# A float32 transpose of 8192 by 8192: buffers split three and two, a looped TensorE, and ScalarE as the issuer

## The chip, the core and the metric

The kernel runs on one core of one Trainium2 chip. The core has a matrix engine (TensorE, PE in the profile), VectorE (DVE), ScalarE (ACT), GpSimd (POOL) and SyncE (SP), each with its own queue of instructions, and 16 DMA engines that move data between the chip's memory (HBM) and the on-chip memory (SBUF). TensorE writes into accumulators (PSUM). The metric is the time of one execution on the device in microseconds, lower is better.

## The reference

```python
"x": np.random.randn(8192, 8192).astype(np.float32)
...
return np.transpose(x)
```

268.4 MB are read and 268.4 MB are written. There is no arithmetic; all of the work is to move data and to turn it.

## The kernel before

The input is cut into 128 chunks, numbered t: two strips of 4096 columns, and in each strip 64 groups of 128 rows. One load brings a chunk, 128 rows by 4096 columns (2 MB), into a unit of SBUF. A unit is 16 pieces of 256 columns; a piece is transposed by two TensorE instructions of 128 by 128, so a chunk is 32 transposes into PSUM, whose two halves (`pss[0]`, `pss[1]`) hold eight pieces each. ScalarE empties the first half and VectorE the second.

A transposed chunk would give output rows that are only 512 bytes long. So the output is put together over 16 chunks. The 16 pieces of a chunk belong to 16 ranges of output rows, numbered q. In step t the range q = t mod 16 is closed: the pieces that chunks t-15 to t have for this range (a window) are brought side by side into a final buffer, and one store of 2 MB writes them, 8 KB a row. Pieces that wait for their range to close lie in `slots`. The first 15 windows, and those at the change from one strip to the other, are shorter or come as two stores; after the last chunk 15 closing windows are left, which are gathered from slots and stored.

SBUF has room for five units. Before the change they are three final buffers (NF = 3) and two load buffers (NIN = 2); the last final buffer takes load 2 at the start and becomes a final buffer from t = 4 on. The work is ordered as follows.

- TensorE (lines 205 to 224) has 28 transposes of the identity ahead of the first chunk (line 207), and then, written out chunk after chunk, the ranges in a turned order: first the range that closes in this step, then the one that closes in the next.
- ScalarE copies the first of these straight from PSUM to the final buffer of this step (line 232) and the second straight to the final buffer of the next step (line 245). Then it copies the other six pieces of its half to slots (line 266).
- VectorE, in step t, first copies its half to slots and, ahead of that in its queue, gathers the 14 older pieces of the window that closes in step t+1 (line 255). A gather waits until the store that used this final buffer before has landed.
- SyncE issues every load and every store (lines 122, 177 and 179). The store of step t waits for ScalarE's first copy (`s_last`) and the gather; a load waits until TensorE has finished the chunk that was in its buffer (line 275).
- After the last chunk, ScalarE and VectorE gather the 15 closing windows in turns (line 288), and SyncE issues their stores.

Of the kernel before, what the change touches and what calls it, by code (L numbers as in the profile page):

```python
# [40 lines left out]
def kernel(  # L41
# [28 lines left out]
    NF = 3  # L70
    NIN = 2
    WARM = 28

    with tc.tile_critical():  # L74
# [7 lines left out]
        s_ld = [nc.alloc_semaphore(f"s_ld{k}") for k in range(NIN + 1)]  # L82
        s_st = [nc.alloc_semaphore(f"s_st{k}") for k in range(NF + NIN)]
        s_pe = nc.alloc_semaphore("s_pe")
        s_last = nc.alloc_semaphore("s_last")
        s_cp = [nc.alloc_semaphore("s_cpa"), nc.alloc_semaphore("s_cpv")]
        s_ga = [nc.alloc_semaphore("s_gaa"), nc.alloc_semaphore("s_gav")]

        chunks = [(s, c) for s in range(M // J) for c in range(CH)]
        T = len(chunks)  # L90
# [12 lines left out]

        def unit(k):
            return units[:, k * UNIT:(k + 1) * UNIT]

        where = []
        for t in range(T):
            if t == NIN:
                where.append((unit(NF - 1), s_ld[NIN], 16))  # L110
            else:
                k = (t if t < NIN else t + 1) % NIN
                n = sum(w[1] is s_ld[k] for w in where)
                where.append((unit(NF + k), s_ld[k], 16 * (n + 1)))
        after = [None] * T
        for t in range(NIN + 1, T):
            after[t] = max(u for u in range(t) if where[u][1] is where[t][1])

        def load(t):
            s, c = chunks[t]  # L120
            dst, sem, _ = where[t]
            nc.sync.dma_start(
                out=dst, in_=x[c * P:(c + 1) * P, s * J:(s + 1) * J]
            ).then_inc(sem, 16)
# [25 lines left out]
        def move(e, o, i):  # L150
            return nc.scalar.copy(out=o, in_=i) if e == 0 else nc.vector.tensor_copy(out=o, in_=i)  # L151


        free = list(range(NF - 1))
# [14 lines left out]
        def store(w):  # L169
            q, r, parts, _, _ = w  # L170
            for s, a, z, base in parts:
                rows = (z - a) * P
                j0 = s * J + q * B * P
                dst = out[j0:j0 + B * P, a * P:z * P].rearrange("(p b) i -> p b i", p=P)
                src = units[:, base:base + B * rows]
                if any(stored):
                    st = wide_dma(nc, nc.sync, "qSPDynamicHW", dst, src)
                else:
                    st = nc.sync.dma_start(
                        out=dst, in_=src.rearrange("p (b i) -> p b i", b=B)  # L180
                    )
                st.then_inc(s_st[r], 16)
                stored[r] += 1
            free.append(r)
# [3 lines left out]
        def gather(e, w, members):  # L188
            eng = (nc.scalar, nc.vector)[e]
            q, r, _, place, before = w  # L190
# [9 lines left out]
        def closing(t):  # L200
            return window(t % W, max(0, t - W + 1), t) if t < T else None

        for t in range(NIN + 1):
            load(t)
        nc.tensor.wait_ge(s_id, 2)
        for k in range(WARM):
            nc.tensor.transpose(pss[1][:, :P], ident, ident)  # L207

        now = closing(0)
        marks = (2, W // 2, W)  # L210
        for t in range(T):
            src, sem, count = where[t]
            nc.tensor.wait_ge(sem, count)
            for i in range(W):
                if t and i % (W // 2) == 0:
                    nc.tensor.wait_ge(s_cp[2 * i // W], t)
                for b in range(B):
                    o = (i % (W // 2) * B + b) * P
                    j = (t + i) % W * PIECE + b
                    tr = nc.tensor.transpose(  # L220
                        pss[2 * i // W][:, o:o + P], src[:, j:j + B * (P - 1) + 1:B], ident
                    )
                if i + 1 in marks:
                    tr.then_inc(s_pe, 1)


            q, r, parts, place, before = now
            if before:
                nc.scalar.wait_ge(s_st[r], before)
            nc.scalar.wait_ge(s_pe, len(marks) * t + 1)  # L230
            off, dist = place[t]
            move(0, view(units, off, 0, 1, dist), view(pss[0], 0, 0, 1, P)).then_inc(s_last, 1)
            need = gathered[1]
            nxt = None
            if t + 1 < T:
                if t + 1 == NIN + 2:
                    free.append(NF - 1)
                while not free:
                    raise RuntimeError
                nxt = closing(t + 1)  # L240
            if nxt:
                if nxt[4]:
                    nc.scalar.wait_ge(s_st[nxt[1]], nxt[4])
                off, dist = nxt[3][t]
                move(0, view(units, off, 0, 1, dist), view(pss[0], PIECE, 0, 1, P))


            if nxt:
                members = [u for u in nxt[3] if u < t]
                if members:  # L250
                    if nxt[4]:
                        nc.vector.wait_ge(s_st[nxt[1]], nxt[4])
                    for k in range(2):
                        nc.vector.wait_ge(s_cp[k], t)
                    gather(1, nxt, members)


            for e in range(2):
                eng = (nc.scalar, nc.vector)[e]
                if need:  # L260
                    eng.wait_ge(s_ga[1], need)
                lo, hi = ((1 if nxt is None else 2), W // 2) if e == 0 else (W // 2, W)
                eng.wait_ge(s_pe, len(marks) * t + 2 + e)  # L263
                pairs = [(slot(t, t + i), (i - e * (W // 2)) * PIECE) for i in range(lo, hi)]
                for a, b, da, db, k in runs(pairs):
                    mv = move(e, view(slots, a, da, k, P), view(pss[e], b, db, k, P))
                mv.then_inc(s_cp[e], 1)

            nc.sync.wait_ge(s_last, t + 1)
            if need:  # L270
                nc.sync.wait_ge(s_ga[1], need)
            store(now)
            for u in range(t + 1, T):
                if after[u] == t:
                    nc.sync.wait_ge(s_pe, len(marks) * (t + 1))
                    load(u)
            now = nxt

        free += [NF + k for k in range(NIN)]
        for q in range(W - 1):  # L280
            w = window(q, T - W + 1 + q, T - 1)
            e = q % 2
            eng = (nc.scalar, nc.vector)[e]
            if w[4]:
                eng.wait_ge(s_st[w[1]], w[4])
            for k in range(2):
                eng.wait_ge(s_cp[k], T)  # L287
            gather(e, w, list(w[3]))
            nc.sync.wait_ge(s_ga[e], gathered[e])
            store(w)  # L290
# [32 lines left out]
```

## Time and profile before

| | |
|---|---|
| median of 3 runs | 1277.04 us (1275.0 to 1277.56) |
| the profiled execution | 1274.58 us, span 1272.8 us |
| TensorE busy, mean granted clock | 741.8 us (58%), 0.755 |
| VectorE, ScalarE busy | 581.1 us (46%), 283.5 us (22%) |
| moved by DMA | 537.53 MB, mean 422 GB/s over the span |
| load of 2 MB, issue to landing | 13.8 us (median) |
| store of 2 MB, issue to landing | 13.0 us (median) |

The page divides the span into 40 slices; a digit is the busy share in tenths, and the line GB/s is what the DMA engines moved in each slice. The chain that ended last is followed back from the last instruction, at each step to what released it. A stage of the answer by windows shows its length, then busy time and instruction count of PE, PE's weight loads, DVE, ACT and POOL, then the granted clock, the share of time that the DMA engines were busy, and GB/s. A line of the order of time has start, duration, engine, line, operation, and in brackets the idle time before it and what ended that.

### The profile page before, as it was taken

What the parts mean: (1) busy time and instruction counts of PE and PEld (TensorE: products, weight loads), DVE (VectorE), ACT (ScalarE), POOL (GpSimd) and SP (SyncE); (2) the same over time, 40 slices, a digit from 0 to 9 for tenths busy, and PEclk for the clock granted to TensorE, in tenths of its full rate; (3) what the DMA queues carried; (4) which work ended last, traced back from release to release, by engine and by line L of the source; (5) the groups of instructions that cost most, each with busy time, mean ns of one, the idle gap of its engine ahead of it and who ended that gap; (6) DMA issues with size and microseconds to landing.
All of it is one profiled execution on the core that took longest, in us unless ns stands there. A gap on an engine that the chain in (4) does not pass through costs nothing.

```text
span 1272.8 us, 10293 instructions
## 1 busy us (share of the span) xinstructions
PE 741.8 (58%) x4124; PEld 717.1 (56%) x4124; DVE 581.1 (46%) x528; ACT 283.5 (22%) x396; POOL 0.7 (0%) x6
## 2 busy tenths in 40 slices
PE   7666556555665566556655556556655665566540
PEld 7556556555564566556654556556655665565530
DVE  2554554445444444544445444444454444544431
ACT  2322112211221122112211212112211221222142
POOL 0000000000000000000000000000000000000000
PEclk9888776877668777777778876877777677768765
DMA  9999999999999999999999999999999999999979
GB/s 375 359 427 430 428 428 431 430 428 428 427 429 429 431 433 427 432 431 429 429 428 426 422 413 427 428 429 430 428 432 429 428 433 429 429 430 430 430 331 396
DMA packets 41358, 537.53 MB, mean 422 GB/s; under 512 B 4576, under 2 KB 5216, under 8 KB 8288
## 3 DMA queue, kind: packets, MB, share of 16 engines
q1 hardware_dynamic: 41312, 536.89, 99.4%
q8 instruction: 32, 0.52, 0.1%
q14 instruction: 14, 0.11, 0.0%
HBM read 268.44 MB, written 268.44 MB: 422 GB/s over the span
## 4 chain that ended last, share of the span: by engine, by line
DMA 69%; PE 28%; ACT 1%; issue 1%; DVE 0%; ACTq 0%; SPq 0%; DVEq 0%
DMA units<-in_x_dram 65%; PE ps L220 28%; DMA out_dram<-units 4%; ACT units L151 1%; DVE slots L151 0%; ACT slots L151 0%; DVE units L151 0%; ACTq L287 0%; DVEq L263 0%; SPq L318 0%; SPq L74 0%; ACTq L230 0%
## 5 line engine op out<-in xcount | busy, mean ns | idle before, releaser
L220 PE MATMUL ps<-ident,units 128*128 128x128 f32 x4096 | 735.7, 361 | 483.2 <-DMA units<-in_x_dram 475.5
L220 PEld LDWEIGHTS ps<-ident,units 128*128 128x128 f32 x4096 | 711.3, 219 | 507.6 <-DMA units<-in_x_dram 499.1
L151 DVE COPY slots<-ps 128x512 f32<-128x512 f32 (+6 forms) x232 | 300.0, 1331 | 629.7 <-PE ps L220 629.7
L151 DVE COPY units<-slots 128x1792 f32<-128x1792 f32 (+7 forms) x296 | 281.3, 997 | 54.5 <-DMA out_dram<-units 37.8
L151 ACT COPY units<-ps 128x256 f32<-128x256 f32 x255 | 82.8, 375 | 734.5 <-PE ps L220 722.6
L151 ACT COPY slots<-ps 128x1536 f32<-128x1536 f32 x128 | 184.4, 1441 | 221.9 <-PE ps L220 221.9
L151 ACT COPY units<-slots 128x2048 f32<-128x2048 f32 (+4 forms) x12 | 15.4, 1326 | 26.3 <-DMA out_dram<-units 22.6
L207 PE MATMUL ps<-ident 128*128 128x128 f32 x28 | 6.1, 415 | 1.7 <-POOL ident L94 1.7
L207 PEld LDWEIGHTS ps<-ident 128*128 128x128 f32 x28 | 5.8, 227 | 1.7 <-POOL ident L94 1.7
L151 ACT ACT_TABLE_LOAD x1 | 1.3, 1283 | 0.9 <-SPq L74 0.9
L94 POOL TENSOR_SCALAR_AFFINE_SELECT ident<-ident 128x128 f32<-128x128 f32 x1 | 0.3, 292 | 0.2 <-POOL ident L92 0.2
L92 POOL MEMSET ident<- 128x128 f32 x1 | 0.2, 204 | 0.5 <-SPq L74 0.5
L307 POOL MEMSET const-bfloat16-1.0<- 128x1 bf16 x1 | 0.1, 101 | 0.0
L307 POOL MEMSET const-uint8-127<- 128x1 uint8 x1 | 0.1, 101 | 0.0
L307 POOL MEMSET const-float32-0.0<- 128x1 f32 x1 | 0.1, 98 | 0.2 <-issue 0.2
L307 POOL MEMSET const-float32-1.0<- 128x1 f32 x1 | 0.1, 98 | 0.0
## 6 DMA issues: line engine op xcount, KB each, us to landing
units<-in_x_dram SPq DMA_DIRECT2D x128, 2048.0 KB, 13.8
out_dram<-units SPq DMA_DIRECT2D x98, 2048.0 KB, 13.0
out_dram<-units SPq DMA_DIRECT2D x4, 1920.0 KB, 11.7
out_dram<-units SPq DMA_DIRECT2D x4, 1792.0 KB, 11.7
out_dram<-units SPq DMA_DIRECT2D x4, 1664.0 KB, 11.4
out_dram<-units SPq DMA_DIRECT2D x4, 1536.0 KB, 12.0
out_dram<-units SPq DMA_DIRECT2D x4, 1408.0 KB, 12.1
out_dram<-units SPq DMA_DIRECT2D x4, 1280.0 KB, 11.5
```

Source lines behind the costliest of these rows:

```text
L92: nc.gpsimd.memset(ident, 0.0).then_inc(s_id, 1)
L94: nc.gpsimd.affine_select(out=ident, in_=ident, compare_op=mybir.AluOpType.not_equal, fill=1.0, base=0, pattern=[[-1, P]], channel_multipl ...
L151: return nc.scalar.copy(out=o, in_=i) if e == 0 else nc.vector.tensor_copy(out=o, in_=i)
L207: nc.tensor.transpose(pss[1][:, :P], ident, ident)
L220: tr = nc.tensor.transpose(pss[2 * i // W][:, o:o + P], src[:, j:j + B * (P - 1) + 1:B], ident)
L307: nc = _bacc.Bacc("TRN2", target_bir_lowering=False, num_devices=1)
```

## The change

The units become two final and three load buffers. Chunk t is always loaded to load buffer t mod 3; the first three loads are issued by SyncE, all others, and all stores, by ScalarE, in the queue that also does its copies. TensorE runs a loop of 43 passes, three chunks each (two in the first), with the ranges in the fixed order 0 to 15; semaphores that it counts down itself tell it that a load has landed (`s_ld`) and that a half of PSUM is free (`s_bank`), and it signals after every fourth range. The warm-up transposes are gone. In step t VectorE gathers all 15 older pieces of window t, and only the piece of chunk t itself goes straight from PSUM, by the engine whose half it lies in. The store waits for that half's copies and for the gather. Closing windows take the load buffers first, and their stores are issued by ScalarE too.

```diff
--- before.py
+++ after.py
@@ -67,9 +67,11 @@
     PIECE = B * P
     SLOTS = W * (W - 1) // 2
     UNIT = W * PIECE
-    NF = 3
-    NIN = 2
-    WARM = 28
+    NH = NR // 2
+    NF = 2
+    NIN = 3
+    MARK = 4
+    MARKS = NR // MARK
 
     with tc.tile_critical():
         nc.alloc_sbuf_tensor("pad", [P, 32], dt)
@@ -79,15 +81,12 @@
         pss = [nc.alloc_psum_tensor(f"ps{k}", [P, UNIT // 2], dt).ap() for k in range(2)]
 
         s_id = nc.alloc_semaphore("s_id")
-        s_ld = [nc.alloc_semaphore(f"s_ld{k}") for k in range(NIN + 1)]
+        s_ld = [nc.alloc_semaphore(f"s_ld{k}") for k in range(NIN)]
         s_st = [nc.alloc_semaphore(f"s_st{k}") for k in range(NF + NIN)]
+        s_bank = [nc.alloc_semaphore("s_banka"), nc.alloc_semaphore("s_bankv")]
         s_pe = nc.alloc_semaphore("s_pe")
-        s_last = nc.alloc_semaphore("s_last")
         s_cp = [nc.alloc_semaphore("s_cpa"), nc.alloc_semaphore("s_cpv")]
         s_ga = [nc.alloc_semaphore("s_gaa"), nc.alloc_semaphore("s_gav")]
-
-        chunks = [(s, c) for s in range(M // J) for c in range(CH)]
-        T = len(chunks)
 
         nc.gpsimd.memset(ident, 0.0).then_inc(s_id, 1)
         nc.gpsimd.wait_ge(s_id, 1)
@@ -101,27 +100,59 @@
             channel_multiplier=1,
         ).then_inc(s_id, 1)
 
+        chunks = [(s, c) for s in range(M // J) for c in range(CH)]
+        T = len(chunks)
+
         def unit(k):
             return units[:, k * UNIT:(k + 1) * UNIT]
 
-        where = []
-        for t in range(T):
-            if t == NIN:
-                where.append((unit(NF - 1), s_ld[NIN], 16))
-            else:
-                k = (t if t < NIN else t + 1) % NIN
-                n = sum(w[1] is s_ld[k] for w in where)
-                where.append((unit(NF + k), s_ld[k], 16 * (n + 1)))
-        after = [None] * T
-        for t in range(NIN + 1, T):
-            after[t] = max(u for u in range(t) if where[u][1] is where[t][1])
-
         def load(t):
             s, c = chunks[t]
-            dst, sem, _ = where[t]
-            nc.sync.dma_start(
-                out=dst, in_=x[c * P:(c + 1) * P, s * J:(s + 1) * J]
-            ).then_inc(sem, 16)
+            (nc.sync if t < NIN else nc.scalar).dma_start(
+                out=unit(NF + t % NIN), in_=x[c * P:(c + 1) * P, s * J:(s + 1) * J]
+            ).then_inc(s_ld[t % NIN], 16)
+
+        def transposes(k):
+            nc.tensor.sem_inc(s_ld[k], -16).wait_op(s_ld[k], 16, "sem-ge")
+            src = unit(NF + k)
+            for q in range(NR):
+                e, g = divmod(q, NH)
+                if g == 0:
+                    nc.tensor.sem_inc(s_bank[e], -1).wait_op(s_bank[e], 1, "sem-ge")
+                for b in range(B):
+                    o = (g * B + b) * P
+                    j = q * PIECE + b
+                    tr = nc.tensor.transpose(
+                        pss[e][:, o:o + P], src[:, j:j + B * (P - 1) + 1:B], ident
+                    )
+                if q % MARK == MARK - 1:
+                    tr.then_inc(s_pe, 1)
+
+        assert T % NIN == NIN - 1
+        pe = [nc.tensor.engine]
+        for e in range(2):
+            nc.tensor.sem_inc(s_bank[e], 1)
+        nc.tensor.wait_ge(s_id, 2)
+
+        turn = nc.alloc_registers("turn", engines=pe)
+        nc.regs_mov(turn, 0)
+        nc.br("turns", engines=pe)
+        with nc.body("turns", valid_engines=pe):
+            now = nc.snap(turn, min_val=0, max_val=T // NIN)
+            with nc.tensor.If(now < 3):
+                hint = nc.tensor.mark_branch_hint_location()
+            with nc.tensor.If(now > 0):
+                transposes(NIN - 1)
+            for k in range(NIN - 1):
+                transposes(k)
+            nc.regs_alu(turn, turn, 1, op=mybir.AluOpType.add)
+            nc.tensor.br_lt(
+                turn, T // NIN + 1, on_true="turns", on_false="done"
+            ).branch_hint(hint)
+        nc.switch_bb("done")
+
+        for t in range(NIN):
+            load(t)
 
         def slot(t, q):
             t, q = t % W, q % W
@@ -150,8 +181,7 @@
         def move(e, o, i):
             return nc.scalar.copy(out=o, in_=i) if e == 0 else nc.vector.tensor_copy(out=o, in_=i)
 
-
-        free = list(range(NF - 1))
+        free = list(range(NF))
         stored = [0] * (NF + NIN)
 
         def window(q, t0, t1):
@@ -174,9 +204,9 @@
                 dst = out[j0:j0 + B * P, a * P:z * P].rearrange("(p b) i -> p b i", p=P)
                 src = units[:, base:base + B * rows]
                 if any(stored):
-                    st = wide_dma(nc, nc.sync, "qSPDynamicHW", dst, src)
+                    st = wide_dma(nc, nc.scalar, "qActDynamicHW", dst, src)
                 else:
-                    st = nc.sync.dma_start(
+                    st = nc.scalar.dma_start(
                         out=dst, in_=src.rearrange("p (b i) -> p b i", b=B)
                     )
                 st.then_inc(s_st[r], 16)
@@ -186,8 +216,10 @@
         gathered = [0, 0]
 
         def gather(e, w, members):
+            q, r, _, place, before = w
             eng = (nc.scalar, nc.vector)[e]
-            q, r, _, place, before = w
+            if before:
+                eng.wait_ge(s_st[r], before)
             groups = {}
             for t in members:
                 groups.setdefault(place[t][1], []).append((slot(t, q), place[t][0]))
@@ -197,96 +229,57 @@
             mv.then_inc(s_ga[e], 1)
             gathered[e] += 1
 
-        def closing(t):
-            return window(t % W, max(0, t - W + 1), t) if t < T else None
-
-        for t in range(NIN + 1):
-            load(t)
-        nc.tensor.wait_ge(s_id, 2)
-        for k in range(WARM):
-            nc.tensor.transpose(pss[1][:, :P], ident, ident)
-
-        now = closing(0)
-        marks = (2, W // 2, W)
         for t in range(T):
-            src, sem, count = where[t]
-            nc.tensor.wait_ge(sem, count)
-            for i in range(W):
-                if t and i % (W // 2) == 0:
-                    nc.tensor.wait_ge(s_cp[2 * i // W], t)
-                for b in range(B):
-                    o = (i % (W // 2) * B + b) * P
-                    j = (t + i) % W * PIECE + b
-                    tr = nc.tensor.transpose(
-                        pss[2 * i // W][:, o:o + P], src[:, j:j + B * (P - 1) + 1:B], ident
-                    )
-                if i + 1 in marks:
-                    tr.then_inc(s_pe, 1)
-
-
-            q, r, parts, place, before = now
-            if before:
-                nc.scalar.wait_ge(s_st[r], before)
-            nc.scalar.wait_ge(s_pe, len(marks) * t + 1)
-            off, dist = place[t]
-            move(0, view(units, off, 0, 1, dist), view(pss[0], 0, 0, 1, P)).then_inc(s_last, 1)
-            need = gathered[1]
-            nxt = None
-            if t + 1 < T:
-                if t + 1 == NIN + 2:
-                    free.append(NF - 1)
-                while not free:
-                    raise RuntimeError
-                nxt = closing(t + 1)
-            if nxt:
-                if nxt[4]:
-                    nc.scalar.wait_ge(s_st[nxt[1]], nxt[4])
-                off, dist = nxt[3][t]
-                move(0, view(units, off, 0, 1, dist), view(pss[0], PIECE, 0, 1, P))
-
-
-            if nxt:
-                members = [u for u in nxt[3] if u < t]
-                if members:
-                    if nxt[4]:
-                        nc.vector.wait_ge(s_st[nxt[1]], nxt[4])
-                    for k in range(2):
-                        nc.vector.wait_ge(s_cp[k], t)
-                    gather(1, nxt, members)
-
-
+            q = t % W
+            w = window(q, max(0, t - W + 1), t)
+            place = w[3]
+            if t:
+                nc.vector.wait_ge(s_cp[q // NH], t)
+                gather(1, w, [u for u in place if u < t])
             for e in range(2):
                 eng = (nc.scalar, nc.vector)[e]
-                if need:
-                    eng.wait_ge(s_ga[1], need)
-                lo, hi = ((1 if nxt is None else 2), W // 2) if e == 0 else (W // 2, W)
-                eng.wait_ge(s_pe, len(marks) * t + 2 + e)
-                pairs = [(slot(t, t + i), (i - e * (W // 2)) * PIECE) for i in range(lo, hi)]
-                for a, b, da, db, k in runs(pairs):
-                    mv = move(e, view(slots, a, da, k, P), view(pss[e], b, db, k, P))
+                if t:
+                    eng.wait_ge(s_ga[1], t)
+                seen = 0
+                ranges = range(e * NH, (e + 1) * NH)
+                straight = [g for g in ranges if g == q]
+                groups = [
+                    (slots, P, u)
+                    for part in ([g for g in ranges if g < q], [g for g in ranges if g > q])
+                    for u in runs([(slot(t, g), (g - e * NH) * PIECE) for g in part])
+                ]
+                if straight:
+                    off, dist = place[t]
+                    groups.append((units, dist, [off, (q - e * NH) * PIECE, 0, 0, 1]))
+                groups.sort(key=lambda g: g[2][1])
+                for base, dist, (a, b, da, db, k) in groups:
+                    mark = t * MARKS + ((b + (k - 1) * db) // PIECE + e * NH) // MARK + 1
+                    if mark > seen:
+                        eng.wait_ge(s_pe, mark)
+                        seen = mark
+                    mv = move(e, view(base, a, da, k, dist), view(pss[e], b, db, k, P))
                 mv.then_inc(s_cp[e], 1)
-
-            nc.sync.wait_ge(s_last, t + 1)
-            if need:
-                nc.sync.wait_ge(s_ga[1], need)
-            store(now)
-            for u in range(t + 1, T):
-                if after[u] == t:
-                    nc.sync.wait_ge(s_pe, len(marks) * (t + 1))
-                    load(u)
-            now = nxt
-
-        free += [NF + k for k in range(NIN)]
-        for q in range(W - 1):
-            w = window(q, T - W + 1 + q, T - 1)
-            e = q % 2
+                eng.wait_ge(s_cp[e], t + 1)
+                eng.sem_inc(s_bank[e], 1)
+
+            nc.scalar.wait_ge(s_cp[q // NH], t + 1)
+            if t:
+                nc.scalar.wait_ge(s_ga[1], t)
+            store(w)
+            if t + NIN < T:
+                nc.scalar.wait_ge(s_pe, (t + 1) * MARKS)
+                load(t + NIN)
+
+        free = [NF + k for k in range(NIN)] + free
+        for n in range(W - 1):
+            q = (T + n) % W
+            w = window(q, T - W + 1 + n, T - 1)
+            e = n % 2
             eng = (nc.scalar, nc.vector)[e]
-            if w[4]:
-                eng.wait_ge(s_st[w[1]], w[4])
-            for k in range(2):
-                eng.wait_ge(s_cp[k], T)
+            eng.wait_ge(s_cp[1 - e], T)
+            eng.wait_ge(s_cp[e], T)
             gather(e, w, list(w[3]))
-            nc.sync.wait_ge(s_ga[e], gathered[e])
+            nc.scalar.wait_ge(s_ga[e], gathered[e])
             store(w)
         for r in range(NF + NIN):
             nc.sync.wait_ge(s_st[r], 16 * stored[r])
```

## The prediction

> **What bounds the kernel now.** I read the page's first lines, its slices and queues first, then the chain that ended last, then the three-microsecond stages at both ends, and last the order of time in the steady part. The page:
>
> ```profile
> span 1272.8 us, 10293 instructions
> DMA  9999999999999999999999999999999999999979
> GB/s 375 359 427 430 428 428 431 430 428 428 427 429 429 431 433 427 432 431 429 429 428 426 422 413 427 428 429 430 428 432 429 428 433 429 429 430 430 430 331 396
> q1 hardware_dynamic: 41312, 536.89, 99.4%
> q8 instruction: 32, 0.52, 0.1%
> DMA 69%; PE 28%; ACT 1%; issue 1%; DVE 0%; ACTq 0%; SPq 0%; DVEq 0%
> ```
>
> The transfer engines are full in all slices but one, at 425 to 433 GB/s; only the first two slices (375, 359) and the last two (331, 396) fall off. The chain shows TensorE at 28%, yet in the middle that is the loop of two load buffers round a full queue: a load is issued when the chunk before it is transposed, and 13.8 us pass to its landing, of which its own 2.10 MB at 430 GB/s are 4.9 us. So time is to be had where the transfers have holes. The stages (transfer share and GB/s last):
>
> ```profile
> 0.00:3.00 3.00, 1.27 (x6) 1.27 (x7) 0.00 (x0) 1.28 (x1) 0.70 (x6) 1.00 0.38 82
> 27.00:30.00 3.00, 2.60 (x22) 2.41 (x21) 1.37 (x2) 0.04 (x1) 0.00 (x0) 1.00 0.90 352
> 30.00:33.00 3.00, 0.61 (x6) 0.42 (x4) 0.69 (x2) 0.69 (x2) 0.00 (x0) 1.00 0.69 220
> 39.00:42.00 3.00, 2.63 (x22) 2.44 (x21) 2.18 (x3) 0.92 (x3) 0.00 (x0) 1.00 0.44 103
> 45.00:48.00 3.00, 0.00 (x0) 0.00 (x0) 2.87 (x4) 0.00 (x0) 0.00 (x0) 1.00 0.88 230
> ```
>
> ```profile
> 1227.00:1230.00 3.00, 0.00 (x0) 0.00 (x0) 2.87 (x2) 0.79 (x1) 0.00 (x0) 0.91 0.28 120
> 1230.00:1233.00 3.00, 0.00 (x0) 0.00 (x0) 3.00 (x4) 3.00 (x3) 0.00 (x0) 0.50 0.00 0
> 1233.00:1236.00 3.00, 0.00 (x0) 0.00 (x0) 0.07 (x1) 3.00 (x3) 0.00 (x0) 0.50 0.78 328
> ```
>
> Against 430 GB/s the 63 us at the start (mean 367) lose 9.3 us: 2.4 before the first byte, 6.9 in later holes. The six stages from 1218 to 1236 (371, 289, 431, 120, 0, 328; mean 256) lose 7.3 us; the tail after 1269 loses 2.0 us. What is left, 1254 us, is transfer at 428.
>
> **The change part by part.** The sum is made against the profiled execution, 1274.58 us (1.8 us round its span), 2.5 us under the median of 1277.04; I subtract from the median.
>
> *Three load buffers from end to end.* Before, the third load buffer becomes a final buffer after the first chunks, and the holes at 39 and 45 us are two load buffers waiting on transposes while stores are still small. Afterwards load t+3 is issued once chunk t is transposed. Following the first chunks with rows (4.9 us a load, 4.1 to 5.6 us for 32 transposes, 2.4 us for DVE's eviction): load 3 is out at about 15 us while the first three loads last to 18; load 4 at 19 against 24; load 5 at 25 against 29. The queue stays some 4 us ahead. I leave 1.5 of the 6.9 us of holes: gain 5.4.
>
> *The warm-up goes.* 28 transposes took 6.1 us, 32 of chunk 0 4.1 us: so some 16 of chunk 0's run slow, 2 us later once. The 4 us of queue cover it: 0; uncovered, 2 us.
>
> *TensorE looped.* 43 passes over one body. Its instruction queue now moves 0.52 MB, 1.2 us at 430 GB/s; I count 1.0 as gained, 0 if each pass is fetched again. No jump back is in the trace. Bound: 0 to the longest wait for issue in front of a transpose, 3.7 us, times 42, or 155 us of TensorE, 1.2 us a chunk. TensorE waited 475.5 us for loads in 124 chunks, 3.8 us each, so it hides: 0 on the path. [...] The new block that all engines enter before the first load: 0 to 3.7 us, I take 0.5 lost (nearest: SP's short waits on TensorE's queue, 0.7 and 0.4 us).
>
> *ScalarE issues.* SP's issues took 0.33 us a load and 0.54 us a store, longest 1.38. On ScalarE that is 0.87 us a chunk, 1.5 where two stores go out, beside 2.1 us of copies (0.65 + 1.44), in a period of 9.75 us. No row shows ScalarE issuing; bounds 0 and 1.38 each, 2.8 us a chunk: still half idle. What queues behind: ScalarE now waits for VectorE's copies before a store of the upper eight ranges, then for chunk t's last transpose before load t+3; its next evictions stand behind. TensorE's next first half takes 2.8 us, so ScalarE, free some 2.4 us after the chunk's end, is in time: 0. SP's queue keeps three loads and the last waits.
>
> *Order fixed, 15 of 16 pieces gathered.* A store was issued 1.6 us after the chunk's first transpose (below: 307.65, 309.22); it now waits for gather and half an eviction, 4 to 8 us. VectorE's gather grows from 14 to 15 pieces (256 more elements, 0.17 us by 1217 ns for 1792), and its eviction has up to 3 parts, as before: 2.6 + 2.4 us of 9.75. Both stay off the path while the queue holds work.
>
> ```profile
> 307.65 5.58 PE L220 MATMUL ps<-ident,units 128*128 128x128 f32 x32 [4.40 <-DMA units<-in_x_dram]
> 309.22 0.54 SPq L28 DMA_DIRECT2D out_dram<-units  x1
> 311.39 1.44 ACT L151 COPY slots<-ps 128x1536 f32<-128x1536 f32 x1 [1.91 <-PE ps L220]
> 313.26 0.33 SPq L122 DMA_DIRECT2D units<-in_x_dram  x1
> 313.34 2.42 DVE L151 COPY slots<-ps 128x512 f32<-128x512 f32 x3 [5.27 <-PE ps L220]
> 315.89 2.42 DVE L151 COPY units<-slots 128x2048 f32<-128x2048 f32 x3
> ```
>
> *Two final buffers.* This is the tightest loop: store t lands, VectorE gathers window t+2 (2.6), both engines evict chunk t+2 (2.4), store t+2 goes out (0.6 with its waits): 5.9 us with signals. Two periods are 19.5, so a store may take 13.6 us to land. Alone it needs 4.9 of data and some 2.5 round it (first load: issued 0.96, chunk begun 8.34), 7.4: 6.2 us remain as queue ahead of it. The loop then closes with the queue never empty: cost 0. What is late next is VectorE, which should wait for a store's landing in nearly every chunk, where it did 8 times.
>
> *The end.* Before, the last chunk lands at 1220.07; VectorE's last eviction ends at 1229.1, and ScalarE needs 3.6 us for the first closing gather (1896 + 1682 ns), so that its store is issued at 1232.72, the queue empty since about 1228. Afterwards, with load 127 landing at L, store 125 (to L+4.9) and store 126 (to L+9.8) still run; gather 127 begins at L+5, eviction ends near L+10, store 127 is issued at L+10 and carries data to about L+16; the closing gather, L+10.5 to L+14.1, lies beside it, and the next one, on VectorE, is done before it. One hole of some 3 us stays instead of 7.3: gain 4.3. Later closing stores wait on ScalarE for VectorE's gathers, 2.2 us at most, under stores of 3 to 4.5 us.
>
> Sum: 5.4 + 1.0 - 0.5 + 4.3 = 10.2 us; 1277.04 - 10.2 = 1267.
>
> **The rivals.** (1) *The holes come back* (no gain): TensorE cold, its clock granted at 0.52 by 21 us, and each early store waiting for gather and eviction, the queue runs dry at the start as before, and the end gains 2 at most. For it: early chunks carry only 5.2 to 6 us of transfer and 32 transposes took 5.6 us. Against: three loads stand ahead. 1275 to 1281. (2) *The store loop binds* (slower): if the landing of stores does not shrink as the queue does. Its place is VectorE's wait ahead of each gather; it decides beyond 13.6 us. Half a microsecond a chunk over 126 chunks is 63 us: 1340. For it: the 2 MB stores already land after 13.0 us, loads after 13.8. Against: most of that is the queue itself, at a transfer share of 1.01, and the shortest landing of all stores and loads is 4.3 us, where little stood ahead. (3) *TensorE's loop stalls* by more than the 3.8 us plus the queue; three chunks need 18 us of 29, so a pass would need over 11 us of stall, three times the longest seen: 12 us would give 30 us a pass, +30 us: 1307. (4) *A deeper queue streams better*: loads alone ran at 437 GB/s (9 to 15 us); half way from 430 is +0.8%, and 1257.
>
> **How the numbers follow.** The forecast (10 gained, some holes more or less) 0.60; rival 4 0.07; rival 1 0.16, of which 0.08 beyond 0.2% slower; rival 2 0.13; rival 3 0.04. A measurement of this kernel tells about 0.2%, 2.6 us, from no change. Faster 0.67, same 0.08, slower 0.25. The likeliest case alone spans 1260 (all holes gone) to 1273. The range goes down to 1257 with rival 4, up to 1284: rival 1, plus the 2 us of the cold clock and 1 of the block entered late; rivals 2 and 3 are left out, 0.17.
>
> **What would show it.** Right: no stage between 24 and 60 us under 400 GB/s; no empty stage near the end; 428 to 432 in the middle; loads landing about 18.5 us after issue (6.2 ahead, a store's 4.9, own 7.4), stores about 13.6; VectorE's waits for stores in over 100 chunks, TensorE's for loads shorter. Wrong: a transfer share under 0.97 in the middle (the store loop or TensorE's passes), store landings above 14 us with holes behind them, ScalarE's issues over 1.4 us, or holes that stay at the start.

## The result, and the profile after

The changed kernel takes 1269.8 us (median of 6 runs) against 1277.3 us: a ratio of 0.9932, 95% interval 0.9907 to 0.9957. The profiled execution took 1271.95 us, its span is 1270.2 us. The forecast was 1267 us, in a range from 1257 to 1284. Some executions of kernels of this family, of the runs below too, were disturbed by over 1.5%; ratios leave those out and are what counts below, above all where a median stands higher.

The page of the changed kernel, in the order in which the page before was read:

```profile
span 1270.2 us, 10834 instructions
DMA  9999999999999999999999999999999999999989
GB/s 387 422 425 425 426 428 431 428 432 429 430 431 432 429 432 431 430 426 427 425 424 421 412 422 431 431 423 424 427 427 424 425 428 430 425 424 427 424 346 390
q10 hardware_dynamic: 40880, 530.60, 98.7%
q1 hardware_dynamic: 432, 6.29, 1.2%
q8 instruction: 1, 0.02, 0.0%
DMA 69%; DVE 14%; ACT 5%; issue 3%; ACTq 1%; PE 0%; DVEq 0%
L182 DVE COPY units<-slots 128x2048 f32<-128x2048 f32 (+7 forms) x304 | 294.5, 1016 | 631.0 <-DMA out_dram<-units 630.2
units<-in_x_dram ACTq DMA_DIRECT2D x125, 2048.0 KB, 19.0
out_dram<-units ACTq DMA_DIRECT2D x98, 2048.0 KB, 14.8
```

The first two slices have come up from 375 and 359 GB/s to 387 and 422; the dip near the end (346) is still there. TensorE has left the chain that ended last; stores and VectorE stand there now. VectorE waits 630 us for stores to land, and a 2 MB store takes 14.8 us to land, a load 19.0, where the forecast had 13.6 and 18.5. The instruction queue has gone from 0.52 to 0.02 MB.

The steady part in order of time. VectorE's gather is released by a landed store; its end releases both engines' evictions, and the store goes out 4.5 us after the landing, followed at once by a load:

```profile
506.16 5.55 PE L125 MATMUL ps<-ident,units 128*128 128x128 f32 x32 [4.30 <-PEq L121]
...
510.99 2.36 DVE L182 COPY units<-slots 128x2048 f32<-128x2048 f32 x2 [5.04 <-DMA out_dram<-units]
513.38 1.65 ACT L182 COPY slots<-ps 128x1792 f32<-128x1792 f32 x1 [7.80 <-DVE units L182]
513.38 2.29 DVE L182 COPY slots<-ps 128x2048 f32<-128x2048 f32 x1
514.93 0.38 ACT L182 COPY units<-ps 128x256 f32<-128x256 f32 x1
515.48 0.56 ACTq L28 DMA_DIRECT2D out_dram<-units  x1
...
516.09 0.60 ACTq L111 DMA_DIRECT2D units<-in_x_dram  x1
```

The stages at both ends of the changed kernel (transfer share and GB/s are last):

```profile
27.00:30.00 3.00, 1.57 (x14) 1.41 (x13) 2.36 (x2) 0.55 (x1) 0.00 (x0) 1.00 0.98 410
30.00:33.00 3.00, 3.00 (x27) 3.00 (x27) 0.69 (x1) 1.71 (x3) 0.00 (x0) 1.00 1.02 437
39.00:42.00 3.00, 2.40 (x19) 2.23 (x18) 0.74 (x1) 1.99 (x3) 0.00 (x0) 0.96 0.93 391
45.00:48.00 3.00, 0.97 (x9) 0.78 (x7) 1.92 (x1) 1.81 (x3) 0.00 (x0) 1.00 0.96 407
...
1212.00:1215.00 3.00, 0.00 (x0) 0.00 (x0) 2.87 (x4) 1.93 (x2) 0.00 (x0) 0.74 0.61 262
1215.00:1218.00 3.00, 2.88 (x14) 2.91 (x15) 0.00 (x0) 0.00 (x0) 0.00 (x0) 0.50 0.82 350
1218.00:1221.00 3.00, 3.00 (x19) 3.00 (x18) 1.06 (x1) 0.00 (x0) 0.00 (x0) 0.62 0.99 426
1221.00:1224.00 3.00, 0.38 (x4) 0.19 (x2) 2.96 (x3) 1.68 (x2) 0.00 (x0) 0.94 0.13 55
1224.00:1227.00 3.00, 0.00 (x0) 0.00 (x0) 2.79 (x5) 1.90 (x2) 0.00 (x0) 0.50 0.41 175
```

The holes at 30, 39 and 45 us are gone; the lowest stage between 24 and 60 us is the one of 391 GB/s, a little under the 400 that the prediction asked for. At the end there are two: one at 1212 to 1218 that the forecast did not have, and one at 1221 to 1227.

For a balance, each stage of 3 us is set against 430 GB/s, and what it falls short of is added up: over the first 63 us, over the last 76 to 78 us, and over what lies between. The runs of the experiments are in the table already.

| kernel | span | start | middle (mean GB/s) | end |
|---|---|---|---|---|
| before, first profile | 1272.8 | 9.3 | 3.8 (428.5) | 9.8 |
| before, second profile | 1273.6 | 9.5 | 4.8 (428.2) | 9.4 |
| changed, first profile | 1270.2 | 3.8 | 8.3 (426.8) | 9.4 |
| changed, second profile | 1266.8 | 3.7 | 4.2 (428.4) | 10.1 |
| before with three load, two final buffers | 1274.0 | 3.6 | 6.7 (427.5) | 13.9 |
| changed, TensorE written out | 1264.6 | 3.6 | 2.3 (429.1) | 8.8 |
| changed, last load buffers used at once | 1266.4 | 3.8 | 5.5 (427.9) | 8.3 |
| changed, both of these | 1264.3 | 3.9 | 3.1 (428.8) | 7.4 |
| changed, queue emptied at step 120 | 1269.4 | 3.7 | 10.8 (425.9) | 6.1 |

From the first profile before to the first after: start -5.5, middle +4.5, end -0.4, and 0.5 MB less code, -1.2; together -2.6, the difference of the spans. The two profiles of the changed kernel differ by 4 us in the middle, the two of the kernel before by 1 us.

### The profile page after: what moved, and what is told of

It is laid out like the page before. It is cut to its first block, busy times and chain, and to the rows that moved or that the text cites. A ratio compares the mean times of both kernels' runs of the same rounds, so it can differ in the third digit from the quotient of the medians.

```text
span 1270.2 us, 10834 instructions
## 1 busy us (share of the span) xinstructions
PE 735.3 (58%) x4096; PEld 714.6 (56%) x4096; DVE 599.0 (47%) x600; ACT 266.1 (21%) x309; POOL 0.7 (0%) x6
## 2 busy tenths in 40 slices
DMA packets 41329, 537.04 MB, mean 423 GB/s; under 512 B 4576, under 2 KB 5216, under 8 KB 8288
## 4 chain that ended last, share of the span: by engine, by line
DMA 69%; DVE 14%; ACT 5%; issue 3%; ACTq 1%; PE 0%; DVEq 0%
DMA out_dram<-units 69%; DVE units L182 9%; DVE slots L182 5%; ACT slots L182 4%; ACT units L182 1%; ACTq L28 1%; PE ps L125 0%; DVEq L222 0%; ACTq L267 0%; ACTq L263 0%; ACTq L222 0%; ACTq L280 0%; DVEq L258 0%
## 5 line engine op out<-in xcount | busy, mean ns | idle before, releaser
L125 PE MATMUL ps<-ident,units 128*128 128x128 f32 x4096 | 735.3, 361 | 486.0 <-PEq L121 486.0
L182 DVE COPY units<-slots 128x2048 f32<-128x2048 f32 (+7 forms) x304 | 294.5, 1016 | 631.0 <-DMA out_dram<-units 630.2
L182 ACT COPY slots<-ps 128x1536 f32<-128x1536 f32 (+7 forms) x232 | 237.2, 1047 | 909.2 <-DVE units L182 896.7
L182 DVE COPY slots<-ps 128x512 f32<-128x512 f32 (+7 forms) x232 | 287.1, 1257 | 32.6 <-PE ps L125 28.6
L182 ACT COPY units<-ps 128x256 f32<-128x256 f32 x64 | 24.2, 377 | 63.6 <-DVE units L182 55.2
L182 DVE COPY units<-ps 128x256 f32<-128x256 f32 x64 | 26.6, 416 | 0.3
## 6 DMA issues: line engine op xcount, KB each, us to landing
out_dram<-units ACTq DMA_DIRECT2D x98, 2048.0 KB, 14.8
```

Of the source, the lines that this page charges most:

```text
L125: tr = nc.tensor.transpose(pss[e][:, o:o + P], src[:, j:j + B * (P - 1) + 1:B], ident)
```

## The experiments

Three theories are told apart. *The queue*, as in the prediction: transfers bound the middle, a store's landing shrinks as the queue does, and holes lie only at the ends. *The store loop*, the second rival: a landing is as long as it is, and what is added to the loop is paid. *The drift*, formed on the result: the traces hold 16 signals for each transfer (4576 for 286 transfers, before and after), the kernels go on at the last, and each is taken as the landing of one engine's share; by the theory the shares of one transfer drift apart, and the queue must cover the distance as well. The trace keeps the time of each signal. From the first to the last of a transfer they lie 3.3 us apart in the first profile before (median), and 6.7 us in the first after. These distances are worked out from the signals; no line of the views shows them.

**The changed kernel once more.**

> The changed kernel once more, for a second profile. Its first profile lost 3.8 us at the start (63 us, against 430 GB/s), 8.3 us in the middle (mean 426.8 GB/s, where the kernel before had 428.5) and 9.4 us at the end. If the middle's 4.5 us are a cost of the change, this profile has a middle under 427.5 GB/s again; if they are chance, it comes out at 428 to 430 and the span some 3 to 5 us shorter. Start and end as in the first profile in either case. Time 1266 to 1272 us.

1268.49 us, ratio 0.9918 (0.9904 to 0.9932). The middle came out at 428.4 GB/s, as before the change. So the 4.5 us that the first profile lost there are not a fixed cost of the change. Start and end are as in the first profile.

**The buffers alone, in the kernel before.**

```diff
-    NF = 3
-    NIN = 2
+    NF = 2
+    NIN = 3
...
-                where.append((unit(NF - 1), s_ld[NIN], 16))
...
+            where.append((unit(NF + t % NIN), s_ld[t % NIN], 16 * (t // NIN + 1)))
...
-    free = list(range(NF - 1))
+    free = list(range(NF))
```

> The kernel before with three load and two final buffers from end to end, nothing else changed (SyncE issues, unrolled TensorE, two pieces straight from PSUM, warm-up). If the start's gain is the third load buffer, the start loses some 4 us instead of 9.3; the end keeps its hole of 7 us; no code is saved: 1271 to 1273 us. If the start's gain came from the other parts, the time stays at 1277.

1274.4 us, ratio 0.9968 (0.9956 to 0.998): 3.5 us are gained. The start loses 3.6 us, as in the changed kernel, so the start's gain is the third load buffer and nothing else of the change. The end lost 13.9 us instead of 9.8, which nobody expected. The signals lie 8.9 us apart there late in the run, more than in any other kernel of the table above.

**Two load buffers in the changed kernel.**

```diff
-    NF = 2
-    NIN = 3
+    NF = 3
+    NIN = 2
...
```

The loop then runs 64 passes of two chunks.

> The changed kernel with two load and three final buffers. By the prediction the holes at the start come back (5.4 us): 1272 to 1276 us. Second theory, that the deeper queue lets the 16 shares of a transfer drift apart (in the changed kernel they land 6.7 us apart at the median, 3.3 before) and that this costs the middle: with two load buffers the spread stays under 5 us and the middle comes back to 428.5 GB/s, so that the time is only some 1 us above the changed kernel, if at all.

1354.05 us, ratio 1.0581 (1.0561 to 1.0601). Both expectations are far off. The holes are not at the start alone:

```profile
GB/s 307 389 347 362 408 431 401 391 405 396 428 421 398 397 419 432 392 402 398 401 398 395 405 374 410 404 384 411 397 405 429 404 419 386 413 429 399 413 344 395
units<-in_x_dram ACTq DMA_DIRECT2D x126, 2048.0 KB, 12.8
out_dram<-units ACTq DMA_DIRECT2D x98, 2048.0 KB, 8.4
```

These are the slices and the issues of its page: the whole run is short of work for the engines. The order of time shows why:

```profile
505.29 5.55 PE L125 MATMUL ps<-ident,units 128*128 128x128 f32 x32 [4.34 <-PEq L121]
...
509.63 0.56 ACTq L28 DMA_DIRECT2D out_dram<-units  x1
...
510.88 0.34 ACTq L111 DMA_DIRECT2D units<-in_x_dram  x1
```

The load for t+2 is issued 5.6 us after the chunk's first transpose here, 5.3 to 6.6 us after it while the early ranges close and 8 to 10 for the upper eight, 7.3 in the mean. And it goes right behind a store, which puts 4.9 us in front of it: 12.8 us to land, which is, as an estimate, 7.6 for itself (a store's landing with the loop 8.4 us longer, below), 4.9 for the store and 0.3. Together 20.1 us in two periods, 10.05 a chunk against 9.8 in the changed kernel; the middle's 403 GB/s are 10.4 a chunk, so a part of the loss, some 0.3 us a chunk, lies beyond these medians. In the kernel before, the store left early and the load some 4 us later (309.22 and 313.26 us in its order of time); with its two load buffers the middle ran at 428.5 GB/s. With the late stores of the change the third load buffer is worth not the 5.5 us at the start alone, but the 84 us that its loss cost (1354.05 against 1269.8).

**SyncE issues.**

```diff
-    (nc.sync if t < NIN else nc.scalar).dma_start(
+    nc.sync.dma_start(
...
-            nc.scalar.wait_ge(s_cp[q // NH], t + 1)
+            nc.sync.wait_ge(s_cp[q // NH], t + 1)
...
-    st = wide_dma(nc, nc.scalar, "qActDynamicHW", dst, src)
+    st = wide_dma(nc, nc.sync, "qSPDynamicHW", dst, src)
```

> All loads and stores go back to SyncE, everything else as changed. By the prediction ScalarE's issues cost nothing: the time is that of the changed kernel within 2.6 us, with the same start, middle and end. Rival: the issues of 0.56 and 0.60 us in ScalarE's queue, or its DMA queue, are what the middle lost: then the middle is back at 428.5 GB/s or more and the time 4 to 5 us below the changed kernel.

Ratio 0.993 (0.991 to 0.995), from two executions of 1269.6 and 1270.3 us. That is the changed kernel (0.9932 and 0.9918). Who issues makes no difference that these times show. That the middle is not won back rests on the time alone; its GB/s were not compared.

**TensorE written out.**

```diff
-        with nc.body("turns", valid_engines=pe):
-            ...
+        for t in range(T):
+            transposes(t % NIN)
```

> The changed kernel with TensorE's 128 chunks written out instead of looped, same order and semaphores. The instruction queue moves 0.5 MB again: by the prediction +1.0 us (1.2 us at 430 GB/s) and nothing else, 1270 to 1272 us. Rival: the loop's jumps cost something that the trace hides, or the block entered late: then it is faster than the changed kernel by over 2.6 us.

1266.99 us, ratio 0.9919 (0.9902 to 0.9936). The 0.5 MB come back (span less losses in the table: 1249.9 us of transfer against 1248.7 in the first profile after) and are not seen in the time: it is not slower than the changed kernel (0.9932 and 0.9918), and the intervals overlap. So neither the predicted 1.0 us nor the rival's cost of the jumps is shown.

**The last load buffers used at once.**

```diff
             if t + NIN < T:
                 load(t + NIN)
+            else:
+                free.insert(0, NF + t % NIN)
...
-        free = [NF + k for k in range(NIN)] + free
```

> The changed kernel, but a load buffer that gets no further load becomes a final buffer at once, ahead of the others in the list, so that the gathers of the last two chunks need not wait for a store to land. By the reading of the trace the end's empty stages (1.75 us at 1212 to 1218, 5.0 us at 1221 to 1227) come from the chain landing of store 125, gather, eviction, store 127: without the wait the end loses 3 to 4 us instead of 9.4, and the time is 5 us under the changed kernel, 1263 to 1266 us. If the hole comes from ScalarE's closing gather of 3.5 us instead, it stays and at most 2 us are gained.

Ratio 0.9913 (0.9896 to 0.9929), some 1267 us against the 1263 to 1266 expected. The end loses 8.3 us, 1.1 to 1.8 less than the changed kernel, where 5 were expected. The last two gathers no longer wait for stores, and there are still two holes in the stages at its end:

```profile
1209.00:1212.00 3.00, 0.00 (x0) 0.01 (x1) 2.85 (x4) 0.00 (x0) 0.00 (x0) 0.77 0.64 273
1212.00:1215.00 3.00, 2.98 (x14) 3.00 (x15) 1.43 (x2) 0.00 (x0) 0.00 (x0) 0.50 1.02 437
1215.00:1218.00 3.00, 3.00 (x18) 3.00 (x17) 0.00 (x0) 1.93 (x2) 0.00 (x0) 0.59 0.79 339
1218.00:1221.00 3.00, 0.41 (x4) 0.22 (x2) 2.36 (x2) 0.00 (x0) 0.00 (x0) 0.98 0.15 66
```

The first begins before load 127 is complete (its chunk begins at 1212.0), while store 125 has been in the queue since 1202.0. The transfer share is 0.64 in that stage: engines are idle while others still work on the load. So it was not the wait that the edit took away. That is what the drift would do.

**The loop made 4 us longer.**

```diff
...
+            if t >= W - 1:
+                held = unit(w[1])
+                for n in range(2):
+                    hd = nc.scalar.copy(out=held[:, :UNIT // 2], in_=held[:, :UNIT // 2])
+                    hd.then_inc(s_hold, 1)
+                    holds += 1
+                    nc.scalar.wait_ge(s_hold, holds)
             store(w)
```

> The changed kernel with two copies of half a final unit onto itself on ScalarE ahead of each store from window 15 on, 1.9 us each: every store goes out some 4.0 us later. By the prediction the store loop had 6.2 us of queue ahead of a store, so the queue shortens and the time stays within 2.6 us; the median landing of a 2 MB store falls from 14.8 to about 10.8 us. By the rival that landings do not shrink, 4 us in every two chunks are 2.0 us a chunk, 126 chunks, 250 us more. By the theory of the drifting shares the slack left, some 3 us, is smaller than the 6.7 us by which the shares land apart, so some engines run empty: a middle 1 to 2% slower, +10 to +25 us.

1302.81 us, ratio 1.0191 (1.0164 to 1.0219): some 34 us over the changed kernel. The landing did shrink, to 11.6 us, so the store loop theory (250 us) falls. But it was not free, which the queue theory had expected, and it cost more than the 10 to 25 us that were expected of the drift. The issues on its page:

```profile
units<-in_x_dram ACTq DMA_DIRECT2D x125, 2048.0 KB, 16.1
out_dram<-units ACTq DMA_DIRECT2D x98, 2048.0 KB, 11.6
```

The middle of its answer by windows:

```profile
360.00:390.00 30.00, 16.58 (x96) 16.09 (x96) 13.97 (x13) 17.11 (x11) 0.00 (x0) 0.83 1.00 412
```

The middle runs at 415 GB/s, with the share of busy engines still at 1.00. The signals lie 4.4 us apart from 300 us on, and no further.

**The loop made 8.4 us longer.** Three such copies, and the gather of full windows done twice:

```diff
...
+            for again in range(1 + twice):
+                if again:
+                    mv.then_inc(s_twice, 1)
+                    doubled[0] += 1
+                    eng.wait_ge(s_twice, doubled[0])
                 for n, pairs in groups.items():
...
```

> Three such copies (5.9 us) and VectorE's gather of full windows done twice (2.5 us): the store loop is 8.4 us longer. That is over the 6.2 us of slack of the prediction by 2.2 us in two chunks, 1.1 us a chunk over some 112 chunks: +120 us, about 1390 us, with store landings at their floor of 7 to 8 us. By the drifting shares more, +150 to +200 us. By the landings that do not shrink 8.4/2 times 112, +470 us. If the loop is not what limits, no change.

1338.16 us, ratio 1.047 (1.0449 to 1.049): 70 us over the changed kernel. The landing has come down to 7.6 us on its page, and a stage of the middle has 406 GB/s:

```profile
out_dram<-units ACTq DMA_DIRECT2D x98, 2048.0 KB, 7.6
```

```profile
360.00:390.00 30.00, 16.08 (x96) 15.59 (x96) 19.75 (x17) 21.77 (x15) 0.00 (x0) 0.83 1.00 406
```

All three expectations were too high. The one of 120 us took the loop beside the landing as 5.9 us. In the changed kernel it is 4.8: two periods of 9.8 less 14.8. With that, the two periods are 7.6 + 4.8 + 8.4 = 20.8, 10.4 a chunk, 0.6 us over 9.8, and 112 chunks give 67 us. So where the queue is used up the loop binds as was worked out, with its own term corrected after the run.

The median spread of the 16 signals late in the run (900 to 1190 us), beside the queue that stands ahead of a store, which is its landing less the 7.6 us of the first row:

```
kernel                                   store lands   ahead   signals apart   middle GB/s
loop + 8.4 us                               7.6         0.0        0.5            404.8
loop + 4.0 us                              11.6         4.0        4.4            415.1
before, first profile                      13.0         5.4        4.6            428.5
changed, first profile                     14.8         7.2        7.5            426.8
changed, second profile                    14.8         7.2        7.5            428.4
before, three load and two final buffers   16.2         8.6        8.9            427.5
```

The 7.6 us are not quite a store alone: store 127 of the changed kernel, issued right behind a stage of 55 GB/s, landed after 6.7 us, and by that every row has 0.9 us more ahead. The share of a store that lands first says the same in another way. Late in the run it lands 7.0 to 7.4 us after the issue in the four kernels where the two columns are nearly equal, so nothing much is left ahead of it, and 8.6 us after it in the first profile before. By the table the shares drift until the distance has used up the queue, in four kernels of quite different queues (0.0, 4.0, 7.2 and 8.6 us ahead, 0.5, 4.4, 7.5 and 8.9 apart); the kernel before had not got so far (5.4 and 4.6). What makes some shares slower isn't settled. Nor is it shown how the loop of 4.0 us then loses 13 GB/s, since the share that lands last still has 4 us ahead of it.

**The queue emptied once, at step 120.** This asks the drift for the end's holes:

```diff
             store(w)
+            if t == T - 8:
+                nc.scalar.wait_ge(s_st[w[1]], 16 * stored[w[1]])
             if t + NIN < T:
```

> The changed kernel with one more wait: after store 120 is issued, ScalarE waits until it has landed before it issues load 123, so that the queue empties once and all engines start together again. If the shares' drift (7.4 us by then) is what keeps the end's holes, the end loses 4 to 6 us instead of 9.4 to 10.1 and the spread of landings after step 120 is under 2.5 us; the wait itself costs 3 to 8 us, so the time is 1266 to 1273. If the end's holes are the chain landing, gather, eviction, store alone, the end still loses 9 to 10 us and the time is 1271 to 1277.

1274.61 us, ratio 0.9973 (0.9956 to 0.999), some 2 us above the range expected: the wait empties the queue for longer than was reckoned, 8.4 us against 430 GB/s between 1155 and 1173. But the end loses 6.1 us where it lost 9.4 and 10.1, and the signals lie 1.3 us apart in it, not 7.3. The hole ahead of the last store's chunk is gone, and one of 3 us stays. Its stages there:

```profile
1212.00:1215.00 3.00, 0.49 (x3) 0.52 (x4) 1.92 (x3) 1.42 (x2) 0.00 (x0) 0.97 1.00 415
1215.00:1218.00 3.00, 3.00 (x16) 3.00 (x15) 0.00 (x0) 0.00 (x0) 0.00 (x0) 0.50 1.02 437
1218.00:1221.00 3.00, 2.06 (x17) 1.87 (x15) 1.79 (x2) 0.00 (x0) 0.00 (x0) 0.97 1.01 431
1221.00:1224.00 3.00, 0.00 (x0) 0.00 (x0) 2.92 (x3) 1.93 (x2) 0.00 (x0) 1.00 0.40 169
1224.00:1227.00 3.00, 0.00 (x0) 0.00 (x0) 2.83 (x3) 2.37 (x2) 0.00 (x0) 0.67 0.62 262
```

Those two stages lack (1 - 169/430) * 3 + (1 - 262/430) * 3 = 3.0 us. That is the hole that the prediction had kept, and the 3 to 4 us by which the end is shorter are put down to the drift.

**Both low edits together, and the kernel before again.**

> The two edits that came out lowest, together: TensorE written out, and the last load buffers used as final buffers at once. The first ended at 1267.0 us, the second lost 8.3 us at the end instead of 9.4 to 10.1. If both hold, 1265 to 1266 us; if the end's 1 to 2 us were chance, 1267.

> The kernel before once more for a second profile, to see how far the table of start, middle and end differs between two profiles of one kernel: start 9 us lost, middle 3 to 5, end 9 to 10.

Together 1266.22 us, ratio 0.9914 (0.9891 to 0.9937), the lowest median of all, below the kernel before for certain; from the changed kernel (0.9932 and 0.9918) and from either edit alone it isn't told apart. The kernel before gave the same table to 1 us.

## Why the prediction was right, and where it was not

*Three load buffers, 5.4 us at the start.* Right: the start loses 3.7 to 3.8 us instead of 9.3 to 9.5, and the buffers alone in the kernel before do the same. What was missed is that the late stores of the change can't do without the third buffer (84 us).

*The warm-up, 0 on the path.* Right: the first two chunks took TensorE 9.6 us for 64 transposes, some 1.4 us more than twice the 4.1 us of before (2 us were reckoned). The first 16 start 213 ns apart, nearly all others of the two chunks 120. No hole follows: the lowest stage between 6 and 60 us has 382 GB/s.

*The loop, 0 on the path, and 1.0 us for its code.* Right in the trace for the path: TensorE waited 486.0 us in 127 stretches, 3.8 us each, as before. No stall at a jump is to be seen on the path: the queue of instructions that moved 0.52 MB in 32 packets before moved 0.02 MB in one for all 43 passes, so nothing shows that the body was fetched again, and written-out code, at 0.9919 against 0.9932 and 0.9918, was neither slower nor provably faster. The 1.2 us of transfer are in the balance of the spans; in the time they could not be shown. The new block cost nothing (first loads at 0.94 us, 0.96 before), not 0.5.

*ScalarE issues, 0.* Right: 0.56 us a store and 0.60 a load in the median, inside the bounds (the longest, 1.46, is over the 1.38), and SyncE in its place gives the same ratio, 0.993.

*Order fixed, 15 of 16 pieces gathered, 0.* Right that gather and eviction, 2.4 and 2.3 us, stay off the path, but the store goes out 9.3 us after the chunk's first transpose (506.16 and 515.48), not 4 to 8, because its gather first waits for a landing.

*Two final buffers, 0.* Right in its result, with VectorE's waits as described (129, 630 us), but mis-sized twice. The loop beside the landing is 4.8 us, not 5.9. And 6.2 us of queue to spare were held for slack, where, by the table above, most of it covers the drift: 4 us taken from it cost 34 us instead of nothing. It came out at no cost with 7.2 us of queue left for shares 7.5 us apart, which is no margin and in part luck. A landing above 14 us with holes behind it was named as a sign of being wrong: 14.8 us it was, but the holes are at the end alone.

*The end, a gain of 4.3 us.* Wrong: 9.8 and 9.4 us lost before, 9.4 and 10.1 after. This is the step that failed. Its chain is right in the trace (load 127 complete at L, store 125 landed at L+4.9, gather to L+7.2, store 127 out at L+9.6), but it ran all engines in step. They were 7.3 us apart: those ahead ran out of work before L (transfer shares of 0.61 and 0.82 from 1212 to 1218), and again ahead of store 127 (0.13 and 0.41 from 1221 to 1227). The signals show it: the first share of store 125 landed at 1212.5 and its last at 1219.8, and store 126 was issued only at 1214.93; its own first share landed at 1221.4, and store 127 was issued at 1224.71. With the drift taken away, the 3 us hole of the prediction is what is left. The order of time there:

```profile
1214.93 0.55 ACTq L28 DMA_DIRECT2D out_dram<-units  x1
1215.12 6.26 PE L125 MATMUL ps<-ident,units 128*128 128x128 f32 x32 [3.74 <-PEq L121]
...
1219.94 2.35 DVE L182 COPY units<-slots 128x1792 f32<-128x1792 f32 x2 [5.03 <-DMA out_dram<-units]
...
1224.71 0.55 ACTq L28 DMA_DIRECT2D out_dram<-units  x1
```

*The middle, no change.* Open to some 4 us. One profile of the changed kernel lost 4.5 us more there, the next 0.4 more than the first profile before. That the drift, once it has used up the queue, makes it vary is only argued; TensorE written out had shares 7.1 us apart and lost least of all. Rival 4, a deeper queue that streams better, is not borne out: loads took 5.2 us longer to land, and the two middles ran at 426.8 and 428.4 GB/s against 428.5 and 428.2.

The sum, 10.2 us, stands against 7.5 in the medians of the first comparison and 0.82% or 10.5 us by the ratio of the second. With the end's 4.3 us gone, the prediction's own terms leave 5.9, so some 1.6 to 4.6 us of the measured gain are not accounted for by the steps that held, about the size by which two profiles of one kernel differ in the middle. That the forecast came so near is therefore in part luck.

## What to carry to other kernels

Before a share of busy time is taken for a full queue, compare how long a transfer takes to land with how long it takes alone (here 14.8 us and 6.7 us for a 2 MB store): the difference is the slack that new waits may use, and part of it may be spent already on shares that don't land together, 7.5 us apart in the changed kernel late in the run. When stores are issued later in a loop, look at what they then stand in front of; with two load buffers a load that followed at once took 12.8 us to land, of which some 4.9 are, as an estimate, the store, and a further load buffer made that bearable here (1269.8 us against 1354.05). At the end of a run, time the chain from the slowest share, but reckon that the shares ahead of it may run out of work earlier; here the first share of store 125 landed 7.3 us before its last.

## What the runs showed of the hardware

The 16 signals of a transfer, which lay 2.8 us apart (median) in the first 300 us of the changed kernel, landed 7.2 us apart between 500 and 600 us and 7.5 late in the run (900 to 1190 us); in the kernel before with three load buffers it was 8.9 us late in the run, and a single emptying of the queue brought them back to 1.3 us. The share of busy engines hides a short queue: between 360 and 390 us it was 1.01 at 431 GB/s in the changed kernel and 1.00 at 406 GB/s with the loop 8.4 us longer. A 16 KB packet took 611 ns in the median in the kernel before and in the changed one. In the changed kernel 0.9% of them took over 650 ns between 100 and 550 us, with the loop 8.4 us longer 10.9%, with a mean of 924 ns; and the packets of all data still filled 99.1% of the 16 engines' span there, against 99.9%, at 402 GB/s against 423. So the shorter queue shows mostly as longer packets, not as gaps; what an engine does in the longer ones isn't shown. A 2 MB store took 6.7 us to land where it was issued right behind a stage of 55 GB/s (store 127), and 7.6 us in the median with the loop 8.4 us longer, of which its data are 4.9 at 430 GB/s.
